# Delta rule's triangular inverse: the transposed tile by VectorE's 32x32 block transposes instead of a third product per level

## Chip, cores and metric

The kernel runs on one core of one Trainium2 chip. The metric is the device time of one execution in microseconds (us); lower is better. TensorE is called PE here (PEld is its weight load), VectorE DVE, ScalarE ACT, GpSimd POOL, SyncE SP (it issues most transfers).

## The reference, cut to what matters

One layer of a hybrid decoder: an input projection, two token mixers (a gated delta rule, GDN, and an mLSTM), their merge, and a product-key expert layer (PEER). The change touches only GDN. Per head and chunk it solves with a unit lower triangular matrix:

```python
def gdn_chunked(q, k, v, g, beta, S0, chunk):
    ...
    kk = jnp.einsum('bhnck,bhnsk->bhncs', k, k)
    lhs = jnp.where(strict, beta[..., :, None] * decay * kk, 0.0) + jnp.eye(chunk, dtype=jnp.float32)
    def solve(rhs):
        return lax.linalg.triangular_solve(lhs, rhs, left_side=True, lower=True, unit_diagonal=True)
    u = solve(beta[..., None] * v)
    w = solve((beta * jnp.exp(G))[..., None] * k)
    ...
```

## The kernel before, in words

The 592 tokens (16 meta tokens, 512 of the prompt, 64 of the samples) go through GDN in six blocks (`BLK`): one of 16 tokens, four of 128, one of 64 samples. `gdn_block` builds for all four heads at once a tile U (the negated strict triangle, transposed) and from it the inverse. Y holds the transposed inverse and X its transpose; both start as identities, copied by POOL. Then come levels m = 1, 2, 4, ... below the block's size (below 8 for the samples). A level doubles the size of the diagonal blocks that are inverted: z = U'X (PE, tile pz, copied to Z by ACT), py = Z'Y and px = Y'Z (PE), and under a mask of the level the new parts of py go into Y and those of px into X (DVE, `copy_predicated`). Level 1 needs no py, and the last level needs no px, since nothing reads X behind it. A block of 128 has seven levels, that of 16 four, that of 64 three. X is a 128x512 tile for four heads; an f32 product of one head is two PE instructions, so a group "pz", "py" or "px" is eight.

In the same program stand the projection's matmuls (`in_chunk`, tile acc, 48 per chunk of weights), which don't depend on the delta rule. A list scheduler orders each engine's instructions by a cost model, and puts acc matmuls between the groups of a level while DVE or ACT work. What it decides is fixed at build time; on the chip each engine runs its list in order. `conv_chunk` and `gate_chunk` read acc out with DVE (tiles ext, cvt, och); `weights` loads and splits the weights (wr, then wh by ACT, wl by DVE). PSUM holds four acc buffers.

Behind GDN come mLSTM blocks, the rest of the projection, branches, merge, scoring, and the experts.

Of the kernel before, what the change touches and what calls it, by code (L numbers as in the profile page):

```python
# [30 lines left out]
H = 4  # L31
# [89 lines left out]
class Net:  # L121
# [482 lines left out]
    def gdn_block(self, bi):  # L604
        nc = self.nc
        mm = nc.tensor.matmul
        s0, n = BLK[bi]
# [21 lines left out]
        U = self.ck("U", [P, H, P])  # L629
        nc.vector.scalar_tensor_tensor(U[:n, :, :n], pk[:n, :, :n], -1.0, d[:n, :, :n], op0=ALU.mult, op1=ALU.mult)  # L630

        Y = self.ck("Y", [P, H, P])
        X = self.ck("X", [P, H, P])
        idb = self.c("ident")[:n, None, :n].to_broadcast([n, H, n])
        nc.gpsimd.tensor_copy(Y[:n, :, :n], idb)
        nc.gpsimd.tensor_copy(X[:n, :, :n], idb)
        top = LS if samp else n
        lev = [m for m in (1, 2, 4, 8, 16, 32, 64) if m < top]
        for m in lev:
            li = m.bit_length() - 1  # L640
            my = self.lvl[:n, 2 * li * P:2 * li * P + n][:, None, :].to_broadcast([n, H, n])
            mx = self.lvl[:n, (2 * li + 1) * P:(2 * li + 1) * P + n][:, None, :].to_broadcast([n, H, n])
            pz = self.pmx.tile([P, H, P], F32, name="pz", tag="mx")
            for h in range(H):
                mm(pz[:n, h, :n], U[:n, h, :n], X[:n, h, :n], start=True, stop=True)
            if m == 1:
                nc.vector.copy_predicated(Y[:n, :, :n], my, U[:n, :, :n])
                nc.vector.copy_predicated(X[:n, :, :n], mx, pz[:n, :, :n])
                continue
            z = self.ck("Z", [P, H, P])  # L650
            nc.scalar.activation(z[:n, :, :n], pz[:n, :, :n], AF.Copy)
            py = self.pmx.tile([P, H, P], F32, name="py", tag="mx")
            for h in range(H):
                mm(py[:n, h, :n], z[:n, h, :n], Y[:n, h, :n], start=True, stop=True)
            if m != lev[-1]:
                px = self.pmx.tile([P, H, P], F32, name="px", tag="mx")
                for h in range(H):
                    mm(px[:n, h, :n], Y[:n, h, :n], z[:n, h, :n], start=True, stop=True)
                nc.vector.copy_predicated(X[:n, :, :n], mx, px[:n, :, :n])
            nc.vector.copy_predicated(Y[:n, :, :n], my, py[:n, :, :n])  # L660

        pt = self.tok(k4, sl, n)
        if not first:
# [1001 lines left out]
```

## Time and profile before

| | |
|---|---|
| median of 3 runs | 1996.18 us (1994.39 to 2000.45) |
| profiled execution, its own time | 1997.74 us |
| its span | 1996.0 us |
| mean granted TensorE clock | 0.984 |
| PE busy | 1917.5 us, 96% of the span |
| DVE busy | 1605.4 us, 80% |
| instructions on PE | 12681 matmuls |

The span runs from the first to the last instruction of the profiled execution; its own time has 1.74 us more around it. A busy share over the whole span is a mean over stages: GDN's levels lie at about 154 to 375 us.

### The profile page before, as it was taken

Reading aid. Unit: us, or ns where it says so; the run is one execution under the profiler, and the core shown is the slowest. Engines: PE = TensorE matmul, PEld = TensorE weight load, DVE = VectorE, ACT = ScalarE, POOL = GpSimd, SP = SyncE. Lnnn points to the kernel's source line nnn. Section 1 sums busy time; section 2 is a strip of 40 time slices with the busy share of each in tenths; the row PEclk is TensorE's granted clock in tenths of the full one; section 3 lists DMA queues with packets and bytes.
Section 4 is the critical chain, followed back from the end, with each engine's and each line's share of the span. In section 5 each row is a group of like instructions: output and inputs, shape, how many; then the busy total and the mean of one; then the engine's idle time right before and its main releaser. Section 6 shows DMA issues by size and latency. Waiting matters only on the chain.

```text
span 1996.0 us, 33789 instructions
## 1 busy us (share of the span) xinstructions
PE 1917.5 (96%) x12681; PEld 1849.1 (93%) x12681; DVE 1605.4 (80%) x3012; ACT 910.9 (46%) x1595; POOL 750.1 (38%) x547
## 2 busy tenths in 40 slices
PE   7999999999999898899999999999999999999997
PEld 7998999888999798899999999999999999998997
DVE  5685666667555679999999998788999798889895
ACT  5542333343323545444776899633333333333332
POOL 1110000201001355434343453366677565656530
PEclk9998999999999999999999999999999999999998
DMA  7354333464645634699899999999999999999991
GB/s 245 110 158 128 102 90 102 123 187 143 212 146 169 196 118 128 231 329 332 319 352 342 373 407 371 374 390 396 401 400 400 396 401 401 400 401 400 401 357 56
DMA packets 219905, 548.22 MB, mean 275 GB/s; under 512 B 31332, under 2 KB 96612, under 8 KB 218076
## 3 DMA queue, kind: packets, MB, share of 16 engines
q1 hardware_dynamic: 163724, 343.90, 48.9%
q0 software_dynamic: 55296, 201.35, 26.1%
q8 instruction: 99, 1.62, 0.3%
q10 hardware_dynamic: 720, 0.80, 0.1%
q14 instruction: 66, 0.54, 0.1%
HBM read 474.89 MB, written 69.77 MB: 273 GB/s over the span
## 4 chain that ended last, share of the span: by engine, by line
PE 32%; DMA 20%; DVE 5%; issue 2%; POOL 0%; ACT 0%; POOLq 0%; DVEq 0%; SPq 0%; ACTq 0%
DMA wr<-in_v 7%; PE pz L137 6%; PE pz L139 6%; PE pz L138 6%; DMA gz<-gz 5%; DMA gr<-in_v,gi 4%; PE py L138 4%; PE py L139 4%; PE py L137 4%; PE pw L1240 2%; DMA wj<-wd 2%; DVE ul L1416 1%; DMA gr<-in_ur,gi 1%; DVE gr L1322 1%; DVE yt L1329 1%
## 5 line engine op out<-in xcount | busy, mean ns | idle before, releaser
L1310 POOL DMA_INDIRECT gr<-in_ur,gi x192 | 307.7, 1603 | 271.4 <-DVE yt L1329 195.4
L1410 ACT ACTIVATE uh<-wr 128x1024 fp32r<-128x1024 f32 x256 | 270.5, 1057 | 239.1 <-PE py L138 118.0
L1310 POOL DMA_INDIRECT gr<-in_v,gi x192 | 286.0, 1490 | 242.0 <-DVE gr L1322 178.9
L138 PE MATMUL py<-al,uh 128*128 128x384 f32 x1024 | 349.1, 341 | 18.4 <-DVE al L1501 18.2
L137 PE MATMUL py<-ah,uh 128*128 128x384 f32 x1024 | 348.2, 340 | 2.3 <-ACT ah L1496 1.8
L139 PE MATMUL py<-ah,ul 128*128 128x384 f32 x1024 | 347.8, 340 | 0.0
L137 PE MATMUL pz<-x2h,uh 128*128 128x384 f32 x1024 | 346.7, 339 | 0.0
L139 PE MATMUL pz<-x2h,ul 128*128 128x384 f32 x1024 | 342.9, 335 | 2.2 <-DVE ul L1416 2.1
L138 PE MATMUL pz<-x2l,uh 128*128 128x384 f32 x1024 | 342.4, 334 | 0.0
L1416 DVE TENSOR_TENSOR ul<-wr,uh 128x1024 fp32r<-128x1024 f32 x256 | 311.6, 1217 | 15.5 <-issue 4.8
L1329 DVE SCALAR_TENSOR_TENSOR yt<-gr,ga,yt 128x1024 f32<-128x1024 f32 x192 | 245.6, 1279 | 18.7 <-DMA gr<-in_v,gi 17.7
L137 PE MATMUL acc<-xnh,wh 128*128 128x296 f32 (+1 forms) x768 | 233.4, 304 | 7.3 <-ACT xnh L296 6.2
L1322 DVE SCALAR_TENSOR_TENSOR gr<-gr,xt 128x1024 f32<-128x1024 f32 x192 | 233.3, 1217 | 5.6 <-DMA gr<-in_ur,gi 5.3
L138 PE MATMUL acc<-xnl,wh 128*128 128x296 f32 (+1 forms) x768 | 233.6, 304 | 0.5 <-DVE xnl L297 0.5
L139 PE MATMUL acc<-xnh,wl 128*128 128x296 f32 (+1 forms) x768 | 232.8, 304 | 0.4 <-DVE wl L133 0.4
L138 PEld LDWEIGHTS py<-al,uh 128*128 128x128 f32 x1024 | 195.0, 190 | 21.8 <-DVE al L1501 21.5
L132 ACT ACTIVATE wh<-wr 128x1024 fp32r<-128x1024 f32 x104 | 109.9, 1058 | 212.5 <-issue 74.0
L137 PEld LDWEIGHTS py<-ah,uh 128*128 128x128 f32 x1024 | 194.9, 190 | 3.8 <-ACT ah L1496 2.9
L139 PEld LDWEIGHTS pz<-x2h,ul 128*128 128x128 f32 x1024 | 192.2, 188 | 3.4 <-DVE ul L1416 3.4
L139 PEld LDWEIGHTS py<-ah,ul 128*128 128x128 f32 x1024 | 194.8, 190 | 0.0
L137 PEld LDWEIGHTS pz<-x2h,uh 128*128 128x128 f32 x1024 | 192.3, 188 | 0.1
L138 PEld LDWEIGHTS pz<-x2l,uh 128*128 128x128 f32 x1024 | 192.4, 188 | 0.0
(427 smaller groups left out, 3559.1 us busy)
## 6 DMA issues: line engine op xcount, KB each, us to landing
wr<-in_u SPq DMA_DIRECT2D x128, 512.0 KB, 7.2
wr<-in_v SPq DMA_DIRECT2D x128, 512.0 KB, 13.2
gz<-gz SPq DMA_DIRECT2D x96, 384.0 KB, 9.8
wr<-in_w_in SPq DMA_DIRECT2D x48, 512.0 KB, 4.0
wd<-wst SPq DMA_DIRECT2D x12, 2048.0 KB, 8.0
wj<-wd SPq DMA_DIRECT2D x96, 256.0 KB, 16.3
wr<-in_w_q SPq DMA_DIRECT2D x32, 512.0 KB, 4.2
wr<-in_w_out SPq DMA_DIRECT2D x16, 512.0 KB, 4.4
```

Of the source, the lines that this page charges most:

```text
L132: self.last_hi = self.nc.scalar.activation(hi, src, AF.Copy)
L137: mm(out, wh, xh, start=start, stop=False)
L138: mm(out, wh, xl, start=False, stop=False)
L139: self.last_mm = mm(out, wl, xh, start=False, stop=stop)
L1240: nc.tensor.matmul(pw[:, u, :], oh[0][:, t], oh[2 + x][:, t], start=x == 0, stop=x == 1)
L1310: nc.gpsimd.indirect_dma_start(out=t, out_offset=None, in_=src, in_offset=bass.IndirectOffsetOnAxis(ap=self.gi[z][:, x, c:c + 1], axis=0))
L1322: nc.vector.scalar_tensor_tensor(t, t, 1.0, xt, op0=ALU.mult, op1=ALU.mult, accum_out=ga[:, c:c + 1])
L1329: nc.vector.scalar_tensor_tensor(yt, t, ga[:, c:c + 1], yt, op0=ALU.mult, op1=ALU.add)
L1410: self.nc.scalar.activation(w, self.raws[s], AF.Copy)
L1416: self.nc.vector.tensor_sub(w, self.raws.pop(s), self.ws[s][0].bitcast(F32))
```

## The change

X is no longer made by a product. Up to level 16 the inverted blocks are no larger than 32, so all of X that is not zero lies in the 32x32 blocks on the diagonal, and there X is Y with each 32x32 block transposed. DVE does this after it has updated Y. Level 32 (only in blocks of 128) keeps its px. Y is made at least 32 wide, and X's identity is not copied.

```diff
-        idb = self.c("ident")[:n, None, :n].to_broadcast([n, H, n])
-        nc.gpsimd.tensor_copy(Y[:n, :, :n], idb)
-        nc.gpsimd.tensor_copy(X[:n, :, :n], idb)
+
+        w = max(n, 32)
+        nc.gpsimd.tensor_copy(Y[:w, :, :w], self.c("ident")[:w, None, :w].to_broadcast([w, H, w]))
...
+            if m == 1:
+                nc.vector.copy_predicated(Y[:n, :, :n], my, U[:n, :, :n])
+                nc.vector.transpose(X[:w, :, :w], Y[:w, :, :w])
+                continue
             pz = self.pmx.tile([P, H, P], F32, name="pz", tag="mx")
             for h in range(H):
                 mm(pz[:n, h, :n], U[:n, h, :n], X[:n, h, :n], start=True, stop=True)
-            if m == 1:
-                nc.vector.copy_predicated(Y[:n, :, :n], my, U[:n, :, :n])
-                nc.vector.copy_predicated(X[:n, :, :n], mx, pz[:n, :, :n])
-                continue
...
-            if m != lev[-1]:
+            if m != lev[-1] and m > 16:
                 px = self.pmx.tile([P, H, P], F32, name="px", tag="mx")
...
                 nc.vector.copy_predicated(X[:n, :, :n], mx, px[:n, :, :n])
             nc.vector.copy_predicated(Y[:n, :, :n], my, py[:n, :, :n])
+            if m != lev[-1] and m <= 16:
+                nc.vector.transpose(X[:w, :, :w], Y[:w, :, :w])
```

The scheduler's lists change from the first GDN block to the end of the mixers; behind that every engine's order is as before.

PE, the second block of 128, around one level, before (acc are the projection's matmuls; each x4 row is the four heads, eight instructions):

```order
L654 MATMUL py<-Y,Z 128x128 x4
L658 MATMUL px<-Z,Y 128x128 x4
L138 MATMUL acc_3342<-xnl_118,wh 128x296
L139 MATMUL acc_3342<-xnh_110,wl 128x296
L137 MATMUL acc_3341<-xnh_111,wh 128x296
L138 MATMUL acc_3341<-xnl_119,wh 128x296
L139 MATMUL acc_3341<-xnh_111,wl 128x296
L137 MATMUL acc_3342<-xnh_111,wh 128x296
L138 MATMUL acc_3342<-xnl_119,wh 128x296
L645 MATMUL pz<-X,U 128x128 x4
```

The same kind of place of the change (the row of py and five more acc rows stand right ahead of these twelve):

```order
L139 MATMUL acc_3416<-xnh_104,wl 128x296
L137 MATMUL acc_3417<-xnh_104,wh 128x296
L138 MATMUL acc_3417<-xnl_112,wh 128x296
L139 MATMUL acc_3417<-xnh_104,wl 128x296
L137 MATMUL acc_3416<-xnh_105,wh 128x296
L138 MATMUL acc_3416<-xnl_113,wh 128x296
L139 MATMUL acc_3416<-xnh_105,wl 128x296
L137 MATMUL acc_3417<-xnh_105,wh 128x296
L138 MATMUL acc_3417<-xnl_113,wh 128x296
L649 MATMUL pz<-X,U 128x128 x4
L139 MATMUL acc_3417<-xnh_105,wl 128x296
L137 MATMUL acc_3416<-xnh_106,wh 128x296
```

The group px is gone, and between py and the next pz stand more acc matmuls than the seven before: twelve at the least in the blocks of 128, and 14 to 22 where DVE has another instruction between its two steps.

DVE, the block of 16, before (k, q, kb belong to this and the next blocks; cvt and ext to the projection):

```order
L648 COPY_PREDICATED X<-lvl,pz 16x4x16
L587 TENSOR_TENSOR decay<-eg,cst 128x512
L617 TENSOR_TENSOR k_1768<-k_1768,bl 128x512
L659 COPY_PREDICATED X<-lvl,px 16x4x16
L660 COPY_PREDICATED Y<-lvl,py 16x4x16
L624 TENSOR_TENSOR kb<-k_1768,kb 128x512
L617 TENSOR_TENSOR q_2007<-q_2007,bl 128x512
L365 SCALAR_TENSOR_TENSOR cvt<-ext,par,cvt 128x616
L659 COPY_PREDICATED X<-lvl,px 16x4x16
L660 COPY_PREDICATED Y<-lvl,py 16x4x16
```

The same place of the change:

```order
L645 STREAM_TRANSPOSE X<-Y 32x4x32
L617 TENSOR_TENSOR k_1752<-k_1752,bl 128x512
L365 SCALAR_TENSOR_TENSOR cvt<-ext,par,cvt 128x616
L624 TENSOR_TENSOR kb<-k_1752,kb 128x512
L617 TENSOR_TENSOR q_1965<-q_1965,bl 128x512
L660 COPY_PREDICATED Y<-lvl,py 16x4x16
L365 SCALAR_TENSOR_TENSOR cvt<-ext,par,cvt 128x616
L662 STREAM_TRANSPOSE X<-Y 32x4x32
L680 TENSOR_TENSOR qd<-q_1965,eg 128x512
L365 SCALAR_TENSOR_TENSOR cvt<-ext,par,cvt 128x616
L660 COPY_PREDICATED Y<-lvl,py 16x4x16
```

The Y update of level 2 moved behind the q product of the second next block, which waits for a transfer (tile bl).

PE, the end of the block of 16 in the change (ptk are PE transposes of k and v):

```order
L137 MATMUL acc_3005<-xnh_104,wh 128x296
L138 MATMUL acc_3005<-xnl_112,wh 128x296
L649 MATMUL pz<-X,U 16x16 x4
L654 MATMUL py<-Y,Z 16x16 x4
L137 MATMUL acc_3064<-xnh_104,wh 128x296
L138 MATMUL acc_3064<-xnl_112,wh 128x296
L649 MATMUL pz<-X,U 16x16 x4
L137 MATMUL acc_3065<-xnh_104,wh 128x296
L138 MATMUL acc_3065<-xnl_112,wh 128x296
L654 MATMUL py<-Y,Z 16x16 x4
L572 MATMUL ptk<-cst_66,k_1653 16x128 x4
```

Before, three to seven acc matmuls stood behind each px or pz of these levels. In the change 16, 12 and 13 stand ahead of these rows from pkk on, only two at a time between them, and 30 between the first pkk of 128 and the pz behind it, where there were none.

## Rows read from the trace of the kernel before

**Rows 1.** The page of the profile: its first lines, and PE's busy tenths and granted clock in 40 slices.
```profile
span 1996.0 us, 33789 instructions
PE 1917.5 (96%) x12681; PEld 1849.1 (93%) x12681; DVE 1605.4 (80%) x3012; ACT 910.9 (46%) x1595; POOL 750.1 (38%) x547
...
PEclk9998999999999999999999999999999999999998
```

**Rows 2.** Busy time of each engine in five stretches (stretch, length, busy us per engine with instructions in brackets; at the end PE's mean granted clock, the DMA engines' share and GB/s).
```profile
core 0: us, PE busy (x) PEld busy (x) DVE busy (x) ACT busy (x) POOL busy (x), PEclk, DMA share, GB/s
140.00:420.00 280.00, 274.35 (x2122) 252.96 (x2120) 178.60 (x307) 89.93 (x139) 30.33 (x46) 0.98 0.38 112
420.00:500.00 80.00, 75.82 (x549) 69.18 (x548) 54.55 (x125) 37.07 (x64) 7.47 (x8) 0.98 0.58 169
500.00:826.00 326.00, 305.75 (x2203) 293.76 (x2202) 225.19 (x827) 136.44 (x251) 100.10 (x49) 0.98 0.52 166
826.00:1411.00 585.00, 581.91 (x3855) 572.21 (x3854) 538.92 (x961) 382.99 (x815) 263.12 (x183) 1.00 0.95 359
1411.00:1996.00 585.00, 550.03 (x3097) 544.43 (x3095) 513.62 (x598) 192.87 (x211) 326.78 (x198) 0.97 0.95 367
```

**Rows 3.** PE's waits in 150 to 420 us, the longest two in total (who waited for whom: us in total, times, longest).
```profile
PE pss L759 <- DVE vm L751: 1.4, 3, 0.5
PE pfin L598 <- DVE on L737: 1.1, 2, 0.6
```

**Rows 4.** Groups of instructions by line and shape in 140 to 420 us (count, busy us, mean ns of one, idle time before them and what ended it).
```profile
L133 DVE TENSOR_TENSOR wl<-wr,wh 128x1024 fp32r<-128x1024 f32 x19 | 23.1, 1215 | 1.8 <-ACT wh L132 1.7
L658 PE MATMUL px<-Z,Y 128*128 128x128 f32 x160 | 21.1, 275 | 0.0
...
L365 DVE SCALAR_TENSOR_TENSOR cvt<-ext,par,cvt 128x616 f32<-128x616 f32 x24 | 20.4, 851 | 0.1
...
L660 DVE COPY_PREDICATED Y<-lvl,py 128x512 f32<-128x512 uint8 x24 | 17.3, 719 | 7.6 <-PE py L654 7.6
L659 DVE COPY_PREDICATED X<-lvl,px 128x512 f32<-128x512 uint8 x20 | 14.8, 740 | 48.7 <-PE px L658 48.7
```

**Rows 5.** Timeline of one level in the second block of 128 (start us, duration us, engine, line, operation, tiles, count).
```profile
230.72 1.16 PE L645 MATMUL pz<-X,U 128*128 128x128 f32 x8
231.64 0.38 PE L138 MATMUL acc<-xnl,wh 128*128 128x296 f32 x1
...
232.63 1.16 PE L654 MATMUL py<-Y,Z 128*128 128x128 f32 x8
233.62 1.06 PE L658 MATMUL px<-Z,Y 128*128 128x128 f32 x8
234.44 0.38 PE L138 MATMUL acc<-xnl,wh 128*128 128x296 f32 x1
234.66 0.30 PE L139 MATMUL acc<-xnh,wl 128*128 128x296 f32 x1
234.72 0.75 DVE L659 COPY_PREDICATED X<-lvl,px 128x512 f32<-128x512 uint8 x1 [3.44 <-PE px L658]
234.79 0.30 PE L137 MATMUL acc<-xnh,wh 128*128 128x296 f32 x1
...
235.34 0.30 PE L138 MATMUL acc<-xnl,wh 128*128 128x296 f32 x1
235.35 0.72 DVE L660 COPY_PREDICATED Y<-lvl,py 128x512 f32<-128x512 uint8 x1
235.52 1.16 PE L645 MATMUL pz<-X,U 128*128 128x128 f32 x8
```

**Rows 6.** Timeline of DVE: three instructions, each of which reads what the one ahead of it wrote.
```profile
102.13 2.63 DVE L365 SCALAR_TENSOR_TENSOR cvt<-ext,par,cvt 128x616 f32<-128x616 f32 x3
```

**Rows 7.** Timeline of PE: a level's group in the block of 16 and in that of 64, with what follows it.
```profile
155.45 0.36 PE L645 MATMUL pz<-X,U 16*16 16x16 f32 x8
155.74 0.40 PE L138 MATMUL acc<-xnl,wh 128*128 128x296 f32 x1
...
366.18 0.68 PE L645 MATMUL pz<-X,U 64*64 64x64 f32 x8
366.79 0.40 PE L138 MATMUL acc<-xnl,wh 128*128 128x288 f32 x1
```

**Rows 8.** Busy time of each engine in three stretches at GDN's start, with the columns of rows 2.
```profile
150.00:160.00 10.00, 9.67 (x100) 8.51 (x100) 5.58 (x16) 3.57 (x7) 0.34 (x2) 1.00 0.79 223
160.00:170.00 10.00, 8.84 (x83) 7.07 (x82) 8.46 (x16) 4.35 (x8) 2.34 (x5) 0.95 0.59 149
170.00:180.00 10.00, 8.31 (x40) 7.63 (x39) 6.29 (x10) 0.60 (x1) 1.14 (x1) 0.53 0.49 142
```

**Rows 9.** Timeline of DVE and PE there: the q product that waits for a transfer, then PE from the last level of the block of 16 to the third pz of the first block of 128 (in brackets the idle time ahead and what ended it).
```profile
161.04 0.69 DVE L617 TENSOR_TENSOR q<-q,bl 128x512 f32<-128x512 f32 x1 [1.44 <-DMA bl<-l2n]
...
162.68 0.36 PE L645 MATMUL pz<-X,U 16*16 16x16 f32 x8 [0.72 <-DVE X L659]
...
168.93 1.98 PE L628 MATMUL pkk<-kb,k 128*128 128x128 f32 x8
171.79 2.04 PE L645 MATMUL pz<-X,U 128*128 128x128 f32 x8 [0.88 <-DVE U L630]
174.65 2.08 PE L645 MATMUL pz<-X,U 128*128 128x128 f32 x8 [0.82 <-DVE X L648]
...
181.21 1.16 PE L645 MATMUL pz<-X,U 128*128 128x128 f32 x8
```

## The prediction

> **What bounds the kernel now.** I read the page first: PE is busy for 96% of the span at a clock that is nearly always full [rows 1]. A share over the span says little about one stage, so the next view is busy time by stretch: while GDN's levels run (140 to 420 us) PE is busy for 274.35 of 280 us, DVE for 179, ACT for 90, POOL for 30 [rows 2]. PE's own waits there confirm it: the two longest in total are 1.4 and 1.1 us [rows 3]. So this stage is bound by the amount of work on PE. The chain of a level (product, copy, product, masked copy) is long, but the scheduler has filled its gaps with acc matmuls that have to be done anyway. A matmul that is removed here shortens the stage by its own time, as long as the gaps still close.
>
> Does the end of the kernel then move? From 826 us on the DMA engines have a share of 0.95, but at 500 to 826 us only 0.52 [rows 2]: nothing of the expert weights is fetched far ahead, since their buffers are freed by PE's earlier work. The late stages should start earlier by what GDN saves, and their order is unchanged. I take 1:1.
>
> **What is removed.** A group of eight instructions costs PE its spacing, not its modelled duration. px starts at 233.62 and the acc behind it at 234.44, 0.82 us; py to px is 0.99, but a group followed by acc takes 0.92 (pz at 230.72, acc at 231.64), so without px the same work ends 0.82 + 0.99 - 0.92 = 0.89 us earlier [rows 5]. Each block of 128 loses the pz of level 1 and the px of levels 2, 4, 8, 16: 5 groups, in four blocks 20, and 20 x 0.89 = 17.8 us. (Check of the count: px has 160 instructions now, that is 20 groups, of which four stay [rows 4].) The block of 16 loses three groups (pz once, px twice) at 0.29 us (155.45 to 155.74), the samples' block two (pz, px) at 0.61 (366.18 to 366.79): 0.9 + 1.2 us [rows 7]. Together **19.9 us of PE work**.
>
> Off the path go one POOL copy of X per block (POOL is busy for 30 of 280 us [rows 2]) and DVE's copies into X.
>
> **What is added.** DVE gets 25 block transposes for 25 copies into X; each of the 20 large ones takes the place of a predicated copy of 0.74 us [rows 4]. No row shows a transpose. Its nearest rows are that copy, one pass over 512 columns, and the split of a weight tile, 1024 columns in 1.215 us [rows 4]; a transpose that works at half rate would be as long as the latter. Below 0.72 I see no reason, since every DVE pass over 512 columns in this stage reads and writes as much. I take 0.74 us and keep 1.2 for the range. [...] No run so far shows which holds.
>
> **What is moved: the chain of a level.** Before, X was ready one predicated copy after px, and the next pz started 0.05 us behind that copy (234.72 + 0.75, pz at 235.52), while Y's update ran beside pz [rows 5]. Now X waits for Y: py's end, Y's copy, transpose. From py's start: 1.16 until py ends, 0.04 to DVE (as from px's end at 234.68 to 234.72), 0.72 for Y, 0.04 to an instruction that reads it (three dependent ones of 0.851 take 2.63 [rows 4, 6]), 0.74 for the transpose, 0.05 to pz: 2.75 us. PE's cover is py, 0.92, then twelve acc: the second starts 0.22 behind the first, the others every 0.136 (234.66 to 235.34 is five steps), and pz 0.18 behind the last (235.34 to 235.52) [rows 5]: 0.92 + 0.22 + 10 x 0.136 + 0.18 = 2.68 us. So a level waits about 0.07 us, 20 times 1.4 us; before, the same gap was also just closed (X at 235.47, pz at 235.52), so a part of that is paid already. I charge **1.0 us**. Where more acc stand in the gap, DVE has a cvt or ext step between Y and the transpose, which is what they cover. The cover has no slack: each 0.1 us that a transpose takes beyond 0.74 costs up to 20 x 0.1 = 2.0 us. That acc matmuls are used up earlier costs nothing: the acc matmuls left behind the last mLSTM block were 371 and are 179, so the stage doesn't run dry.
>
> **The opening.** GDN's start is the one place where PE is not full. [...] From 168.93 to 181.21 PE does pkk, pz, pz, py, px and eleven acc: at full clock 5 x 0.89 + 11 x 0.136 = 5.9 us, with about 0.5 for changes between kinds 6.4. It takes 12.3 [rows 9]. So 5.9 us are lost there, and 0.7 ahead of the pz at 162.68 [rows 9].
>
> In the change 30 acc lie between pkk and its pz, so the waits of 0.88 and 0.82 go. But the block of 16 gets worse: Y's update of level 2 stands on DVE behind the q product that waited for a transfer until 161.04 [rows 9]. It ends at 161.73; with Y, cvt (0.85 [rows 4]) and transpose X is there at about 162.8. PE has by then done what stands ahead: behind pkk and the first 5 acc, which lead to 155.45 before [rows 7], 36 acc (4.9 us) and two small groups (0.4 each with the changes), and is idle from about 161.1. Two levels follow with two acc between their groups, each with a DVE and an ACT step, until the ptk at about 165.9. In these 4.8 us PE has four groups of 0.29 and four acc, 1.7 us: 3.1 are lost. Queued behind the waiting products on PE are acc matmuls of the next chunk, and behind Y on DVE the ext that frees their PSUM. [...] The opening thus loses 3.1 to 6.5 instead of 6.6: a gain of 0 to 3.5, and I take **2 us**.
>
> Past SP's queue two loads of projection weights move ahead of bl and kb rows that are wanted a block later; hidden by the levels between.
>
> **Sum.** -19.9 + 1.0 - 2 = -20.9 us. Against the profiled execution's own 1997.74 that is 1976.8; the median of the runs is 1.6 lower, 1996.18, and from it I forecast **1975 us**.
>
> **Rivals.**
> 1. *The transpose takes about 1.2 us.* For: it is an untried operation that reorders across partitions. Against: it moves 512 columns like the copies of 0.69 to 0.74. Then 20 x 0.46 = 9.2 us come back: 1984. [...]
> 2. *The gaps stay open for other reasons.* The spacing comes from a cost model, not from this chip; with 0.3 us of wait in each of 20 gaps and nothing won in the opening, -19.9 + 6 = -14: 1982 to 1986. For: no slack in the cover. Against: before, the same model's gaps closed within hundredths [rows 5].
> 3. *The gain is absorbed later:* transfers end the late stages, whose DMA share is 0.95 [rows 2], and don't start earlier. 1996. Against: the 0.52 before them.
> 4. *Slower:* the transpose works at a quarter rate. From 512 to 1024 columns a DVE pass grows by about 0.5 us, so four passes are about 2.2 us; 20 x 1.5 = 30 come back, -21 + 30: about 2005. It decides from a transpose of 0.74 + 21 / 20 = 1.8 us on. Nothing in the profile speaks for it, except that no transpose is in it.
> 5. *More is won:* the opening keeps its clock and level 1's shorter chain saves changes between kinds of products as well: 1968 to 1970; this is the near end of my own case.
>
> **How the numbers follow.** My case, 1967 to 1980, has 0.68; rival 1 (1980 to 1987) 0.12; rival 2 0.08; rival 3 0.05; rival 4 0.05; below 1967 0.02. The range 1966 to 1985 holds my case and most of rivals 1 and 2, about 0.82. The runs before spread by 0.3%, and that is also about what a measurement of this kernel tells from no change. Faster than 1990 are my case, rivals 1 and 2 and what lies below, 0.88 after rounding down for what I don't see; the same 0.07, slower 0.05.
>
> **What would show it.** Right: px with 32 instructions in blocks of 128, transposes of 0.7 to 0.8 us, no wait of pz for the transpose over some tenths, PE still at about 98% in GDN, and the stages from 500 us on shifted by some 20 us with their lengths kept. The opening: an idle PE at about 161 to 166, no waits between pkk and the third pz. Wrong: transposes over 1 us with PE waiting for X at every level; a stretch from 826 us to the end that has grown by what GDN saved; or a granted clock near 0.5 for ten us again.

## The result, and the profile after

The changed kernel takes 1981.15 us (median of 4 runs, 1979.32 to 1983.43); runs of the kernel before beside it had a median of 1996.95. The ratio is 0.9918 (95% interval 0.9900 to 0.9935), 16 us faster. A later measurement gave 0.9928 (0.9905 to 0.9952). The forecast of 1975 had the direction; of its 20.9 us some 16 arrived. The profiled execution took 1983.43 us, 1.83 around its span.

The first lines of the page after, and the granted clock in 40 slices:

```profile
span 1981.6 us, 33367 instructions
PE 1896.2 (96%) x12481; PEld 1826.9 (92%) x12481; DVE 1608.7 (81%) x3012; ACT 909.8 (46%) x1595; POOL 744.2 (38%) x541
...
PEclk9999999999999999999999999999999999999998
```

Against [rows 1] PE has 200 matmuls fewer and 21.3 us less busy time, and the shares are as they were. The page doesn't say where the missing 5 us are. The groups of 140 to 420 us by line and shape come next, the answer to [rows 4]:

```profile
L649 PE MATMUL pz<-X,U 128*128 128x128 f32 x192 | 26.8, 282 | 0.5
L660 DVE COPY_PREDICATED Y<-lvl,py 128x512 f32<-128x512 uint8 x24 | 17.6, 735 | 32.7 <-PE py L654 32.7
L662 DVE STREAM_TRANSPOSE X<-Y 128x512 f32<-128x512 f32 x16 | 11.3, 708 | 0.3
L658 PE MATMUL px<-Z,Y 128*128 128x128 f32 x32 | 4.2, 275 | 0.0
```

px has 32 instructions left of 160. A transpose takes 0.708 us, a little less than the copy next to it. PE shows 0.5 us of idle time in all ahead of the 24 large pz groups. One level shows what lies behind that (answer to [rows 5]):

```profile
179.62 1.16 PE L654 MATMUL py<-Y,Z 128*128 128x128 f32 x8
180.53 0.38 PE L137 MATMUL acc<-xnh,wh 128*128 128x296 f32 x1
180.75 0.30 PE L138 MATMUL acc<-xnl,wh 128*128 128x296 f32 x1
180.81 0.75 DVE L660 COPY_PREDICATED Y<-lvl,py 128x512 f32<-128x512 uint8 x1 [1.65 <-PE py L654]
...
181.59 0.71 DVE L662 STREAM_TRANSPOSE X<-Y 128x512 f32<-128x512 f32 x1
...
182.12 0.29 PE L139 MATMUL acc<-xnh,wl 128*128 128x296 f32 x1
182.45 0.46 PE L649 MATMUL pz<-X,U 128*128 128x128 f32 x2
```

X is ready at 182.30 and the next pz starts at 182.45. This 0.15 us is no slack. In a level with more acc, where X is ready at 192.36, pz starts 0.14 behind the last acc:

```profile
192.77 0.30 PE L139 MATMUL acc<-xnh,wl 128*128 128x296 f32 x1
192.91 0.60 PE L649 MATMUL pz<-X,U 128*128 128x128 f32 x4
```

Above it is 0.33, and 0.15 behind the transpose, as in 15 of the 20 levels that follow a transpose. So the chain ends last there, by up to 0.2 us, and twelve acc (180.53 to 182.12) just fail to cover it. The idle time of 0.5 us doesn't hold this, since it counts from the modelled end of the acc. What pz starts later than one spacing (0.136 us) behind the last acc is 2.4 us over all large levels of the change and 0.9 before.

**Where the time went.** The two programs put different amounts of acc work into each stage, so the time of a milestone alone says little. I count an acc matmul at 0.1363 us (0.136 in [rows 5], 0.137 in the ten steps from 180.75 to 182.12) and take from each part those that it holds. The milestones are one row each, here of before and then of after: the first pkk of GDN, the pkk of the second block of 128 and of the samples, the last py, the last pfin of the mLSTM, the last product of the merge's first loop.

```profile
154.28 0.29 PE L628 MATMUL pkk<-kb,k 128*16 128x16 f32 x5 [0.33 <-DVE kb L624]
221.50 0.28 PE L628 MATMUL pkk<-kb,k 128*128 128x128 f32 x1
364.45 0.27 PE L628 MATMUL pkk<-kb,k 128*64 128x64 f32 x1
373.07 0.27 PE L654 MATMUL py<-Y,Z 64*64 64x64 f32 x1
512.04 0.27 PE L598 MATMUL pfin<-cst,on 64*128 64x64 f32 x1
613.68 0.28 PE L139 MATMUL pbr<-oh,wl 128*128 128x256 f32 x1
```

```profile
151.65 0.21 PE L628 MATMUL pkk<-kb,k 128*16 128x16 f32 x2 [0.29 <-DVE kb L624]
221.71 0.28 PE L628 MATMUL pkk<-kb,k 128*128 128x128 f32 x1
369.19 0.27 PE L628 MATMUL pkk<-kb,k 128*64 128x64 f32 x1
377.67 0.27 PE L654 MATMUL py<-Y,Z 64*64 64x64 f32 x1
517.38 0.27 PE L598 MATMUL pfin<-cst,on 64*128 64x64 f32 x1
598.83 0.28 PE L139 MATMUL pbr<-oh,wl 128*128 128x256 f32 x1
```

The acc matmuls still to come at these six are 1477, 1294, 840, 809, 371, 0 before and 1477, 1217, 627, 588, 179, 0 after. GDN before is thus 373.07 - 154.28 - 668 x 0.1363 = 127.7 us, after 377.67 - 151.65 - 889 x 0.1363 = 104.8. All profiles read this way (us; "left" are the acc matmuls behind the last pfin):

| profile | GDN | mLSTM | last pfin to end of first merge loop | left | ratio (95%) |
|---|---|---|---|---|---|
| before | 127.7 | 79.3 | 51.1 | 371 | 1 |
| before, four raw tiles (e7) | 128.2 | 77.0 | 51.1 | 371 | 1.0000 (0.9987 to 1.0012) |
| after | 104.8 | 84.0 | 57.0 | 179 | 0.9918 (0.9900 to 0.9935) |
| after again (e5) | 103.6 | 83.2 | 54.9 | 179 | 0.9928 (0.9905 to 0.9952) |
| dead px (e1) | 119.1 | 78.5 | 51.5 | 227 | 0.9975 (0.9958 to 0.9991) |
| two transposes (e2) | 106.3 | 80.5 | 59.1 | 83 | 0.9953 (0.9936 to 0.9970) |
| two transposes, four raw tiles (e11) | 105.9 | 83.4 | 55.7 | 83 | 0.9933 (0.9916 to 0.9950) |
| four raw tiles (e3) | 103.7 | 82.5 | 51.7 | 179 | 0.9912 (0.9890 to 0.9934) |
| the same again (e6) | 103.8 | 81.4 | 51.7 | 179 | 0.9899 (0.9878 to 0.9920) |
| block of 16 as before (e4) | 110.8 | 78.6 | 51.4 | 275 | 0.9908 (0.9885 to 0.9931) |
| qs on GpSimd (e8) | 103.5 | 80.3 | 51.5 | 237 | 0.9902 (0.9882 to 0.9923) |
| opening on GpSimd (e9) | 100.7 | 78.8 | 51.5 | 227 | 0.9871 (0.9853 to 0.9890) |
| both (e10) | 100.7 | 80.4 | 51.5 | 237 | 0.9874 (0.9856 to 0.9893) |

So GDN won 22.9 us, more than forecast; the mLSTM part lost 4.7 and the merge's start 5.9. The last merge product is 14.9 us earlier; 2.6 of these were there ahead of GDN already (154.28 against 151.65; over all profiles the first pkk lies at 150.96 to 154.28, in no order of the kernels, so I take it for chance), and 22.9 - 4.7 - 5.9 makes the other 12.3. From there to the end little changes: the spans differ by 14.4 us.

The merge's start: ACT and PE after, then PE's busy time, count and clock in two stretches (columns of [rows 2]):

```profile
541.42 0.29 PE L139 MATMUL acc<-xnh,wl 128*128 128x288 f32 x1
542.68 0.68 ACT L132 ACTIVATE oh<-oraw 128x576 fp32r<-128x576 f32 x1 [2.24 <-DMA oraw<-spo]
543.27 1.04 ACT L132 ACTIVATE wh<-wr 128x1024 fp32r<-128x1024 f32 x1
544.99 0.61 PE L137 MATMUL pbr<-oh,wh 128*128 128x320 f32 x1 [3.27 <-ACT wh L132]
```

```profile
545.00:551.00 6.00, 6.00 (x23) 6.00 (x24) 2.18 (x3) 1.01 (x2) 0.95 (x1) 0.50 0.53 190
551.00:555.00 4.00, 4.00 (x33) 4.00 (x33) 1.52 (x4) 0.72 (x1) 0.00 (x0) 1.00 0.00 0
```

The acc matmuls run out at 541.42. The first merge product needs wh, which stands on ACT behind a copy that waits for a load into one of two raw tiles (oraw). Then the clock is 0.50 for 6 us: 23 matmuls, which at the pace of the next 4 us (33) take 2.8. The wait (3.27, where before had 0.6) costs 2.7 and the clock 3.2: together the 5.9 us of the table.

### The profile page after: what moved, and what is told of

It reads as the page before. It is cut to its first block, busy times and chain, and to the rows that moved or that the text cites. A ratio compares the mean times of both kernels' runs of the same rounds, so it can differ in the third digit from the quotient of the medians.

```text
span 1981.6 us, 33367 instructions
## 1 busy us (share of the span) xinstructions
PE 1896.2 (96%) x12481; PEld 1826.9 (92%) x12481; DVE 1608.7 (81%) x3012; ACT 909.8 (46%) x1595; POOL 744.2 (38%) x541
## 4 chain that ended last, share of the span: by engine, by line
PE 29%; DMA 22%; DVE 5%; issue 3%; POOL 1%; ACT 0%; POOLq 0%; SPq 0%; DVEq 0%; ACTq 0%
DMA wr<-in_v 8%; PE pz L137 6%; PE pz L139 6%; PE pz L138 6%; DMA wj<-wd 5%; DMA gr<-in_v,gi 3%; PE py L138 3%; PE py L139 3%; PE py L137 3%; DMA gz<-gz 3%; DMA gr<-in_ur,gi 2%; PE pw L1242 2%; POOL gr L1312 1%; DVE ul L1418 1%; DVE yt L1331 1%
## 5 line engine op out<-in xcount | busy, mean ns | idle before, releaser
L1418 DVE TENSOR_TENSOR ul<-wr,uh 128x1024 fp32r<-128x1024 f32 x256 | 313.0, 1223 | 15.4 <-issue 6.6
L138 PEld LDWEIGHTS py<-al,uh 128*128 128x128 f32 x1024 | 194.9, 190 | 24.2 <-DVE al L1503 24.1
```

Of the source, the lines that this page charges most:

```text
L138: mm(out, wh, xl, start=False, stop=False)
L1418: self.nc.vector.tensor_sub(w, self.raws.pop(s), self.ws[s][0].bitcast(F32))
```

## The experiments

Theory A: GDN is bound by PE's work, so the removed products are the gain; what is missing went where the merge starts, since GDN's gaps use up acc matmuls that covered the loads there. Rivals: the chain of a level bounds (B), the missing time is chance or absorbed late (C), it is lost in the mLSTM (D). Theory E, on the opening, comes with e9.

**e1: the removed products come back, unread.** The change, with px of levels 2 to 16 computed too:

```diff
-            if m != lev[-1] and m > 16:
+            if m != lev[-1]:
                 px = ...
                     mm(px[:n, h, :n], Y[:n, h, :n], z[:n, h, :n], start=True, stop=True)
+            if m != lev[-1] and m > 16:
                 nc.vector.copy_predicated(X[:n, :, :n], mx, px[:n, :, :n])
```

> The changed kernel with the px products of levels 2 to 16 computed again at their old place but read by nobody (X still comes from the transposes): 16 groups of 128, two of 16 and one of 64 come back on TensorE, level 1's pz stay out. Theory A (GDN is bound by the amount of TensorE work): 16 x 0.89 + 2 x 0.29 + 0.61 = 15.4 us slower than the changed kernel, so about 1996; a few us less if the acc matmuls that are then left for the mixers' end (227 behind the last mLSTM block instead of 179) shorten the wait there: 1991 to 1997. Theory B (the chain of a level bounds GDN and the shorter chain made the gain): the dead products stand beside VectorE's two steps and cost nothing: 1981 to 1984.

Measured: 1989.36 us against 1994.17 before, 0.9975; to the changed kernel's 0.9918 that is 11 us more. Its groups show the 160 px instructions again:

```profile
L658 PE MATMUL px<-Z,Y 128*128 128x128 f32 x160 | 21.1, 275 | 0.0
```

GDN is 14.3 to 15.5 us longer than in the two profiles of the change (15.4 expected). The merge's start loses nothing with 227 acc matmuls left, and the mLSTM part is about 5 us shorter too; so only 11 us are back in total. 1989.36 lies below the 1991 to 1997 that were expected, beside a kernel before that takes 1994.17 here. Theory B falls; the gain in GDN is PE's work.

**e2: each transpose twice.**

```diff
-                nc.vector.transpose(X[:w, :, :w], Y[:w, :, :w])
+                [nc.vector.transpose(X[:w, :, :w], Y[:w, :, :w]) for _ in range(2)]
```

> The changed kernel with each block transpose done twice, into the same tile: TensorE's work is the same, each level's chain is 0.71 us longer, and the scheduler, which knows it, puts more acc matmuls into the gaps (83 are left behind the last mLSTM block instead of 179). Theory A with its second part (what is lost against the forecast is lost where the merge starts, since too few acc matmuls are left there to cover the loads of the branches): GDN itself keeps its length to within 2 us, TensorE waits no longer in the levels, and the first merge product waits some 5 to 12 us longer than the 3.3 us of the changed kernel, up to the 13 us that 96 acc matmuls take: 1986 to 1994. Theory B (chain, or transposes, bound the levels): 20 x 0.71 = 14 us slower with TensorE waiting in front of the pz groups: 1995. Theory C (what was lost has nothing to do with acc matmuls used up): 1981 to 1983.

Measured: 1985.89 us, 0.9953, 7 us more than the change. The large groups of pz and of transposes in 140 to 430 us:

```profile
L649 PE MATMUL pz<-X,U 128*128 128x128 f32 x192 | 26.8, 283 | 0.3
...
L662 DVE STREAM_TRANSPOSE X<-Y 128x512 f32<-128x512 f32 x32 | 22.6, 705 | 0.6
```

The chain of every level is 0.7 us longer and PE waits no more than in the change: the scheduler put more acc into the gaps. GDN grew by 1.5 to 2.7 us. The bill comes at the merge: 59.1 us with 83 acc left, 2 to 4 more than the change. But it doesn't come as expected. The first merge product waits 0.9 us, less than the 3.3 of the change and not 5 to 12 more; the other waits, 3.2 us, stand ahead of the products behind it, which need tiles of the branches. Most of the 96 acc's 13 us was not lost. Theory A's second part holds in direction only.

**e3, e6, e7, e5: four raw tiles for the branches, in the change twice, in the kernel before as the control, and the change again beside them.**

```diff
-            t = op.tile([P, NT], F32, name="oraw", tag="ld", bufs=2)
+            t = op.tile([P, NT], F32, name="oraw", tag="ld", bufs=4)
```

> The changed kernel with four instead of two buffers for the branches' raw tile (oraw), so that four loads can be under way and ScalarE's copies of the merge's first weights don't stand behind a load. Theory A, second part (about 5 us are lost where the merge starts: a wait of 3.3 us of the first merge product and a clock that falls after it): the wait goes, the first merge product starts 3 to 5 us earlier, and the kernel takes 1976 to 1979. Rival C (the 5 us are the spread of the runs, or the late stages absorb them): 1980 to 1982, though the wait is gone. Rival D (the merge's start waits for something else): 1981 with a wait of the same size.

> The changed kernel once more, on the same chip as the next three. By its first runs 0.9918 of the time before (0.9900 to 0.9935). In its profile the part from GDN's first product to its last level was some 23 to 24 us shorter than before, counted with acc matmuls at 0.136 us each; the mLSTM part 3 to 5 us longer; the part from the last mLSTM block to the last merge product 6 us longer. Theory A expects the same three parts again; if they were chance, the second and third are within 1 us of those before.

> Four raw tiles for the branches in the changed kernel, a second time, now beside the changed kernel on one chip. Theory A, second part: the first merge product doesn't wait for ScalarE and the merge starts at full clock, 3 to 6 us less than the changed kernel, ratio to the kernel before 0.988 to 0.990. Rival C (absorbed later): the ratio of the changed kernel, 0.9915 to 0.992.

> The control: the kernel before with four raw tiles for the branches. There 371 acc matmuls stand behind the last mLSTM block and the merge starts without a wait. Theory A, second part: no change, 0.999 to 1.001, since the loads are covered anyway. If four buffers are simply better (a rival to the reading of the run before this one): 0.997 to 0.998, as much as in the changed kernel.

Measured: e3 1977.72 us, 0.9912; on another chip e5 (the change) 1979.21, 0.9928, e6 1976.05, 0.9899, e7 1995.06, 1.0000. PE's first merge product in e6, and 540 to 560 us of e5 and of e6:

```profile
540.72 0.38 PE L137 MATMUL pbr<-oh,wh 128*128 128x320 f32 x1 [0.60 <-issue]
```
```profile
540.00:560.00 20.00, 17.75 (x121) 17.55 (x120) 11.41 (x20) 6.38 (x8) 0.96 (x1) 0.91 0.54 173
```
```profile
540.00:560.00 20.00, 19.40 (x146) 19.31 (x146) 11.83 (x20) 5.13 (x6) 0.95 (x1) 1.00 0.65 218
```

The wait is gone, the clock stays full, and the part is 51.7 instead of 54.9 to 57.0 us. The same edit does nothing in the kernel before, which had cover to spare. The cause at the merge is shown. In total time its size is less sharp: 0.9928 to 0.9899 is 5.8 us, but the medians of e5 and e6 differ by 3.2, the intervals overlap, and e3's ratio alone would say 1 us.

**e11: two transposes and four raw tiles.** The edits of e2 and e3 together.

> Two transposes per level and four raw tiles together. 83 acc matmuls are left behind the last mLSTM block, 11 us, which is less than the loads and splits of the branches need even with four tiles. Theory A, second part: of the 8 us by which the part from the last mLSTM block to the last merge product was longer with two transposes (59.1 against 51.1), some 3 to 6 go, 1979 to 1983. If that part was longer because of the clock or anything in the levels: no change, 1985 to 1986.

Measured: 1982.65 us, 0.9933, inside the 1979 to 1983 that were expected, though its interval overlaps that of e2. The merge's start went from 59.1 to 55.7: 3.4 us came back, as expected. The rest stays: behind the last of the 83 acc PE still waits 2.5 us, now for the branches' tile oh, which fits too little cover.

**e4 and e9: the opening, once with the old products for the block of 16, once with the products that wait for bl taken off VectorE's queue.** e4 keeps level 1's pz and the px for n == 16. e9 has four raw tiles and:

```diff
-            nc.vector.tensor_tensor(x4[:, :, sl], x4[:, :, sl], pr[:, :, :n], op=ALU.mult)
+            (nc.gpsimd if bi in (1, 2) else nc.vector).tensor_tensor(x4[:, :, sl], x4[:, :, sl], pr[:, :, :n], op=ALU.mult)
```

> The changed kernel with the block of 16 tokens done as before (its X from products), the other blocks with transposes. TensorE's work grows by 3 small groups, 0.9 us. The acc matmuls left behind the last mLSTM block are 275 instead of 179. Theory A, second part: the merge starts without a wait, 4 to 5 us are won there, and in the opening the waits at 160 to 163 us (2.8 us) go while those at the first block of 128 may come back (up to 6 us): 1976 to 1983. Rival C (neither the opening nor the cover at the mixers' end matters): 1982. By the forecast that the acc matmuls used up cost nothing: 1981 to 1985, by the opening alone.

> The changed kernel with four raw tiles, and with the products of k and q with their rows (tile bl) on GpSimd for the first two blocks of 128. In the changed kernel they stand in VectorE's queue ahead of the block of 16's Y and wait 2.4 us for a transfer; here no product that waits for bl stands there, and 19, 11, 6, 3, 9 and 4 acc matmuls lie between the small groups instead of 16, 12, 13, 0, 2, 2. Theory E (the waits of 2.8 us and the half clock behind them in the opening come from that queue): the waits at 160 to 163 us fall below 1 us, the clock stays up, and the part from GDN's first product to its last level is 2 to 4 us shorter than in the run with four raw tiles (103.6 us with acc matmuls at 0.136 each): ratio 0.988 to 0.989. Rival: the small groups wait for their own chain, whatever stands in VectorE's queue, or wait for GpSimd: within 1 us, 0.990.

Measured: e4 1977.62 us, 0.9908; e9 1970.99, 0.9871. PE in the opening, after and then e9 (columns of [rows 2], answer to [rows 8]), and PE's waits after (answer to [rows 9]):

```profile
160.00:170.00 10.00, 8.32 (x63) 6.41 (x64) 8.13 (x17) 2.50 (x5) 1.73 (x5) 0.66 0.60 163
170.00:180.00 10.00, 10.00 (x75) 9.54 (x75) 8.29 (x13) 2.34 (x4) 0.78 (x3) 1.00 0.55 161
```
```profile
160.00:170.00 10.00, 10.00 (x95) 8.46 (x93) 8.01 (x16) 4.24 (x8) 4.43 (x7) 1.00 0.82 205
```
```profile
160.55 0.36 PE L649 MATMUL pz<-X,U 16*16 16x16 f32 x8 [1.71 <-DVE X L662]
161.27 0.36 PE L654 MATMUL py<-Y,Z 16*16 16x16 f32 x8 [0.36 <-ACT Z L651]
162.40 0.62 PE L137 MATMUL acc<-xnh,wh 128*128 128x296 f32 x1 [0.77 <-DVE ext L352]
```

In e9 only 0.6 us of the waits for X is left, the clock stays at 1.00, and GDN is 3 us shorter than with four raw tiles alone; theory E holds. Its mLSTM part is also 2.6 us shorter than e6's, which I had not expected: there pfin waits 3.3 us instead of 5.2. In e4 the opening is as before, and worse: half clock comes back at the first block of 128,

```profile
170.00:180.00 10.00, 7.29 (x31) 6.64 (x30) 8.16 (x13) 0.60 (x1) 0.20 (x1) 0.50 0.57 170
```

GDN costs 6 to 7 us more than in the change, and with 275 acc left the mLSTM part and the merge's start lose nothing. The two effects cancel: the same total by another split.

**e8 and e10: the mLSTM.** e8 is four raw tiles and the product qs on GpSimd, e10 that and e9's edit.

```diff
-            nc.vector.tensor_tensor(qs[:, :, :n], q4[:, :, sl], qs[:, :, :n], op=ALU.mult)
+            nc.gpsimd.tensor_tensor(qs[:, :, :n], q4[:, :, sl], qs[:, :, :n], op=ALU.mult)
```

> The changed kernel with four raw tiles, and with the product of q and its row (qs, tile kb) in the mLSTM blocks on GpSimd instead of VectorE. There this product of the next block stands in VectorE's queue ahead of the last steps of the present block and waits for its transfer (2.64 us in the changed kernel), so TensorE's pfin group waits for the tile on (6.2 us in three waits, 3.9 before). Theory D (the mLSTM part is longer because of this wait): the waits of pfin fall below 2 us in total, the mLSTM part becomes 3 to 5 us shorter, 3 to 5 us less than the run with four raw tiles. Rival: GpSimd's product takes several us itself and the wait moves to pn, 0 to +4 us.

> The edits of the run before this one and of the one with qs on GpSimd together, with four raw tiles. If the parts add (opening 2 to 4 us, mLSTM 1 to 2 us, merge 3 to 6 us against the changed kernel): 1969 to 1974, ratio 0.986 to 0.988. If the scheduler's other placement eats one of them: 0.989 to 0.990.

Measured: e8 1973.82 us, 0.9902, no less than e6 within the intervals; e10 1972.08, 0.9874, as e9. PE's longest wait in the mLSTM part, after and in e8 (3.9 us in all before):

```profile
PE pfin L598 <- DVE on L844: 6.2, 3, 2.6
```
```profile
PE pfin L598 <- DVE on L844: 2.8, 2, 1.6
```

The wait halves, but not to below 2 us as theory D said, and the part gets only 1.1 to 2.2 us shorter than in e3 and e6, not 3 to 5. e10's total lies where the parts were expected to add, but the mLSTM part adds nothing to it (80.4 against e9's 78.8).

Most of the rest of the mLSTM part is the clock. The stretches of 20 us in it that are not at 1.00, in before and then two of after:

```profile
460.00:480.00 20.00, 17.77 (x126) 16.99 (x124) 12.94 (x34) 9.04 (x13) 2.55 (x2) 0.91 0.35 107
```
```profile
440.00:460.00 20.00, 16.12 (x116) 15.37 (x115) 13.13 (x32) 9.93 (x18) 0.11 (x1) 0.91 0.51 140
460.00:480.00 20.00, 17.45 (x127) 16.95 (x127) 11.27 (x29) 9.94 (x21) 3.62 (x3) 0.91 0.54 142
```

A clock of 0.91 over 20 us costs 1.8 us of full speed. Counted so from 380 us on, the part loses nothing in e1, e4 and e7, 1.8 us in before, e2, e6 and e9, 3.6 in after, e3, e5, e8 and e10, and 5.4 in e11. The waits of pfin for on (the view above) are 3.9 us in before, 3.3 in e7 and e9, 6.2 in after, 5.7 in e5, 5.2 in e6, 5.1 in e3, 4.0 to 4.5 in e1, e2, e4 and e11, 2.8 in e8 and e10. Take both off the part, and 73.5 to 74.5 us are left in each of the 13 profiles, whose parts run from 77.0 to 84.0. e8 saves 2.4 us of wait against e6, and one more fall of the clock takes 1.8 back. Why the clock falls once more or less often stays open: a wait of 2.05 us in before (465.80) brought a fall, to 0.66 from 465 to 470 us, while in e8 a wait of 1.60 (460.79) brought none, and there the spacing of acc went from 0.13 to 0.24 us at 395.80, where the longest wait in the 20 us ahead is 0.47.

## Why the prediction was right in direction and 5 us too hopeful

**PE's work bounds GDN: right.** e1 shows it. **19.9 us of work removed: right.** The three later blocks of 128 took 221.50 to 364.45 with 454 acc, 81.1 us, and take 221.71 to 369.19 with 590, 67.1: 14.0 less for 15 groups, 0.93 each where the forecast had 0.89. The samples' block won 1.2 (forecast 1.2).

**A transpose at 0.74 us: right, it is 0.708,** a little below the 0.72 under which the forecast saw no reason to go; the predicated copy of that size beside it takes 0.735. The rivals of 1.2 us and of a quarter rate fall with it.

**1.0 us of waits in the levels: right in size.** By the spacing behind the last acc the large levels wait 2.4 us where before they waited 0.9, 1.5 more. From py to pz it is 2.83 us (179.62 to 182.45) where the forecast had a chain of 2.75 and a cover of 2.68; its step from X to pz, taken as 0.05, is 0.15 behind a transpose. That each further 0.1 us would cost up to 2.0 us holds at most for a fixed list: where the scheduler knows the longer chain, 0.7 us more per level cost GDN 1.5 to 2.7 us (e2), and of these the three later blocks of 128 only 0.5 (67.5 against 67.1 and 67.0).

**The opening, 2 us (0 to 3.5): right in size, half right in mechanism.** From the first pkk to that of the second block of 128, less acc, it was 42.3 us and is 34.6 (33.4 in e5); 5.3 of it is removed work (5 x 0.89 and 3 x 0.29), so 2.4 to 3.6 is the opening's. PE did idle at 160 to 163, for 2.84 us where I had 3.1, and the third pz of 128 waits no more. But the product that waited on DVE was k's, not q's:

```profile
156.71 0.69 DVE L617 TENSOR_TENSOR k<-k,bl 128x512 f32<-128x512 f32 x1 [2.39 <-DMA bl<-l2n]
...
159.30 0.21 DVE L660 COPY_PREDICATED Y<-lvl,py 16x64 f32<-16x64 uint8 x1
```

The clock did fall behind the wait, to 0.66 over ten us, which costs 3.4 us of full speed; over the same ten us e5 has 0.83, 1.7 us. The forecast's 6.5 us of loss has 3.4 us in it for such a fall, the author's estimate, which no run ahead of it shows; these 3.4 and 1.7 are what the runs showed in its place.

**"That acc matmuls are used up earlier costs nothing": wrong, and this is the step that failed.** I looked only at whether the stage runs dry: 179 matmuls are 24 us. But behind the last mLSTM block the branches' loads (seven of eight), their splits and the first merge weights have to pass through two raw tiles and through ACT, and that took 26 us (517.38 to 543.27). With 371 acc this was covered; with 179 PE waits 3.3 us and then runs 6 us at a clock of 0.50. It cost 5.9 us in the first profile and 3.8 in e5, and four raw tiles remove it.

**The mLSTM unchanged: wrong by 4 to 5 us.** I gave this part no term of its own, though its list is drawn up anew. Of the 4.7 us in the first profile 2.3 are longer waits of pfin (6.2 against 3.9) and 1.8 a second fall of the clock. With before's own order the part is 77.0 us where the clock doesn't fall (e7) and 79.3 where it does, so about 2 us of such a difference are chance.

**The later stages follow 1:1: right,** 14.9 us at the end of the merge's first loop, 14.4 at the end of the span. The terms for GDN were small rather than large: it won 22.9 to 24.1 us where the sum had 20.9, and the two losses outside it took more than that surplus. The change with four raw tiles and with the opening's products off VectorE's queue (e9) takes 1970.99 us, 0.9871, less than both kernels.

## What to carry to other kernels

Independent work that fills gaps is a stock, and whoever shortens a chain by spending more of it must look at who drew on it last: count what is left against the loads that it still has to cover. When a scheduler places filler, compare stages by time less filler, not by milestones, and look at the granted clock of a stage before you call a remainder unexplained. Here a wait of 3.27 us in front of the merge's products was followed by 6 us at a clock of 0.50, which cost 3.2 us more; with four buffers there instead of two the wait was 0.60 and the clock 1.00 (e6).

## What the runs showed of the hardware that was not expected

A 32x32 block transpose of 128x512 in f32 costs VectorE 0.708 us, less than the 0.735 of a predicated copy of that size. At two places the clock about doubled the loss at a wait: 3.27 us of wait at the merge brought 6 us at 0.50, and 2.84 us in the opening 0.66 over ten us (0.83 in e5); in e6, without the wait, the first of these stretches ran at 1.00, and in e9 the second. That was not so at every wait: in the mLSTM part of before the clock stayed at 1.00 behind a wait of 1.11 us (450.60) and fell to 0.66 over five us behind one of 2.05 (465.80). PE's pz started 0.15 us behind the end of a transpose in 15 of 20 levels of the change, and 0.05 to 0.06 behind that of a predicated copy in 21 of 24 levels before. And GpSimd took 1.3 to 2.0 us for a product for which VectorE takes 0.69, which cost nothing that shows in PE's waits. The two groups on GpSimd in e9 (shortest, median and longest in ns, first and last start, form):

```profile
L617 POOL TENSOR_TENSOR q<-q,bl x2: 1346/1484/1622, 153.5 to 163.2; 128x512 f32<-128x512 f32 x2
L617 POOL TENSOR_TENSOR k<-k,bl x2: 1332/1658/1984, 158.4 to 168.3; 128x512 f32<-128x512 f32 x2
```
